# A hand-written TensorE order for the DeltaNet of a two-layer decoder trunk

## The chip, the cores and the metric

The kernel runs on one core of a Trainium2 chip. The metric is the device time of one execution in microseconds (us). The engines are named as in the profile: PE is TensorE (PEld its weight loads), DVE is VectorE, ACT is ScalarE, POOL is GpSimd, SP is SyncE, which issues most transfers. Each engine works through its own instructions in order and waits on semaphores for the others.

## The reference

Two layers, a gated DeltaNet and a latent attention, each followed by a dense SwiGLU block, all modulated by a conditioning vector (adaLN). SEQ and D_MODEL are 1024, batch 1, everything float32. The change lies in the DeltaNet of the first layer, 8 heads of 128. Cut to what matters:

```python
def gdn_mixer(h, w_in, conv_w, a_log, dt_bias, norm_g, w_out):
    proj = h @ w_in                      # per head: q, k, v, gate; and a, b for decay and beta
    qkv = jax.nn.silu(causal_depthwise_conv(qkv, conv_w))
    ...
    o = chunk_gated_delta_rule(q, k, v, g, beta)
    o = rmsnorm(o, norm_g) * jax.nn.silu(gate)
    return o.reshape(B, T, GDN_VALUE_DIM) @ w_out

def chunk_gated_delta_rule(q, k, v, g, beta):   # S_t = exp(g_t)(I - b_t k_t k_t^T) S_{t-1} + b_t k_t v_t^T
    L = jnp.where(strict, jnp.einsum("bhnid,bhnjd->bhnij", kb, k) * decay, 0.0)
    A = L + jnp.eye(C)
    u, w = triangular solves of A against v * beta and kb * exp(g_cum)
    attn = jnp.einsum("bhnid,bhnjd->bhnij", q, k) * decay
    def step(S, xs):                             # one chunk
        v_new = u_i - w_i @ S
        o_i = q_i @ S + a_i @ v_new
        S = S * gl_i + k_i^T @ v_new
```

## The kernel before

The normed and transposed input stays in SBUF, split into a high and a low fp32r half (hThi, hTlo). Each head has four projections: KT, QT, VT and ZT (the gate). One of them is 48 matmuls: two halves of 512 tokens, 8 contraction tiles, and the three products high·high, high·low, low·high (`mm3`, L195). They are written here as pj, the tile that takes them. Behind each half ACT and DVE do the convolution (taps cacc, L334) and the SiLU. The weights come as one 512 KB transfer into one of three buffers wraw; ACT makes the high half (L177), DVE the low one (L178).

The recurrence uses chunks of 128 tokens, 8 to a head. What a head needs ahead of it is prepared in two steps. `gdn_prep_a` forms K·K (L375), on DVE the sums for the norm of k (junk, L379), on POOL a power (rk), and the matrix L (L392). `gdn_prep_b` solves with L: copies of its diagonal blocks (Ld, L412, four on ACT), 31 substitution steps of two small operations on DVE (L421, L423), then per four chunks a merge: ACT copies Xs (L441), DVE makes U (L443), and four groups of matmuls follow (L447, L452, L462 with L464, L471) with copies between them. It also forms the products Q·K (L433), which DVE multiplies with the decay (at, L434).

`gdn_rec` is the recurrence. A chunk transposes K and V (L488, L489), then: K·S and Q·S (L496, L497); DVE forms r (L499); U·r (L506); ACT copies y (L508); kd·y (L511); DVE updates S (L515); at·y (L518); DVE adds to o (on, L520). Behind every fourth chunk the four pieces of o are scaled (L532), transposed (L537), gated (oT, L539) and written to DRAM. So K·S, U·r and kd·y are the links of a chain, with another engine between each two.

Around this lie the vectors of the adaLN for later phases (an ada step is one 1024-wide DVE operation, L119, behind one 512 KB transfer) and `gdn_out`, the output product of heads 0 to 3: 192 matmuls of 512 columns, each row of tokens reading o back from DRAM.

The order of all engines is the Tile scheduler's. `gdn` writes the work as tokens, A and B for the two preparations, K and V for two projections each, R for the recurrence:

```python
pre, loop, tail = "A0 V0 B0 K1 A1 V1", "B1 R0 K2 A2 V2", "B6 R5 K7 A7 V7 G0 B7 R6"
```

The loop is repeated for five heads, with the numbers raised by one each time, and the last head's R stands inside `gdn_out`. The scheduler then interleaves the instructions of neighbouring tokens on every engine by its own estimate of when each becomes ready.

Of the kernel before, what the change touches and what calls it, by code (L numbers as in the profile page):

```python
# [19 lines left out]
P = 128  # L20
# [12 lines left out]
class Trunk:  # L33
# [188 lines left out]
    def gdn_gates(self, hi, lo, pool, ps):  # L222
# [65 lines left out]
        self.split(gl, self.ghi, self.glo)  # L288
        pg = ps.tile([P, 3, N], F32, name="c")
# [11 lines left out]
    def gdn_proj(self, h, names, hi, lo, res, first=None):  # L301

        nc = self.nc
        for nm in names:
            t = {"KT": 1, "QT": 0, "VT": 2, "ZT": 3}[nm]
            ch = t * 8 + h
            if not first:
                whi, wlo = self.gdn_w(h, nm)
            o = self.gq_pool.tile([P, T], F32, name=nm, bufs=2 if nm == "ZT" else 3)
            prev = None  # L310
            for s in range(2):

                pj = first[nm][s] if first else self.pp.tile([P, 512], F32, name="pj")
                sl = slice(s * 512, s * 512 + 512)
                if not first:
                    self.mm3(pj, [(whi[:, kt], wlo[:, kt]) for kt in range(KT)],
                             [(hi[:, kt, sl], lo[:, kt, sl]) for kt in range(KT)])
                if nm == "ZT":
                    acc = self.gw.tile([P, 512], F32, name="cacc", bufs=2)
                    nc.scalar.activation(out=acc, in_=pj, func=AF.Copy, scale=0.5)  # L320
                    nc.scalar.activation(out=o[:, sl], in_=pj, func=AF.Tanh, scale=0.5)
                    nc.vector.scalar_tensor_tensor(out=o[:, sl], in0=o[:, sl], scalar=1.0, in1=acc, op0=ALU.add,
                                                   op1=ALU.mult)
                    continue
                cr = self.gw.tile([P, 515], F32, name="cr", bufs=2)
                if s == 0:
                    nc.gpsimd.memset(cr[:, 0:3], 0.0)
                else:
                    nc.gpsimd.tensor_copy(cr[:, 0:3], prev[:, 512:515])
                nc.scalar.copy(cr[:, 3:515], pj)  # L330
                acc = self.gw.tile([P, 512], F32, name="cacc", bufs=2)
                nc.scalar.activation(out=acc, in_=cr[:, 3:515], func=AF.Copy, scale=self.cw[:, 3, ch:ch + 1])  # L332
                for j in (2, 1, 0):
                    nc.vector.scalar_tensor_tensor(out=acc, in0=cr[:, j:j + 512], scalar=self.cw[:, j, ch:ch + 1],  # L334
                                                   in1=acc, op0=ALU.mult, op1=ALU.add)

                nc.scalar.activation(out=o[:, sl], in_=acc, func=AF.Tanh)
                nc.vector.scalar_tensor_tensor(out=o[:, sl], in0=o[:, sl], scalar=1.0, in1=acc, op0=ALU.add,
                                               op1=ALU.mult)
                prev = cr  # L340
            res[nm] = o
        return res
# [20 lines left out]
    def gdn_prep_a(self, h, kq):  # L363

        nc, v = self.nc, self.nc.vector
        K, Q = kq["KT"], kq["QT"]
        qq = self.gs.tile([P, NT], F32, name="qq", bufs=3)
        rkb = self.gs.tile([P, NT], F32, name="rkb", bufs=3)
        c2 = self.gs.tile([P, NT], F32, name="c2", bufs=3)
        L = self.gb.tile([P, NT, P], F32, name="L", bufs=2)  # L370
        for qd in range(2):
            pk = self.pc.tile([P, 4, P], F32, name="c")
            for i in range(4):
                cs = slice((qd * 4 + i) * P, (qd * 4 + i + 1) * P)
                nc.tensor.matmul(pk[:, i], K[:, cs], K[:, cs], start=True, stop=True)  # L375
            kd = self.gs.tile([P, 4], F32, name="kd")
            for i in range(4):
                junk = self.gw.tile([P, P], BF16, name="junk")
                v.scalar_tensor_tensor(out=junk, in0=pk[:, i], scalar=1.0, in1=self.ident, op0=ALU.mult,  # L379
                                       op1=ALU.mult, accum_out=kd[:, i:i + 1])  # L380
            v.tensor_scalar(out=kd, in0=kd, scalar1=EPS, op0=ALU.add, scalar2=None)
            rk = self.gs.tile([P, 4], F32, name="rk")
            self.rpow(rk, kd)
            ms = slice(qd * 4, qd * 4 + 4)
            gsl = slice(h * NT + qd * 4, h * NT + qd * 4 + 4)
            v.tensor_tensor(out=rkb[:, ms], in0=rk, in1=self.beta[:, gsl], op=ALU.mult)
            b2 = self.gs.tile([P, 4], F32, name="b2")
            v.tensor_tensor(out=b2, in0=rk, in1=rkb[:, ms], op=ALU.mult)
            v.scalar_tensor_tensor(out=c2[:, ms], in0=b2, scalar=-1.0, in1=self.eg[:, gsl], op0=ALU.mult, op1=ALU.mult)
            dec = self.gdn_decay(h, qd, False, "dec")  # L390
            for i in range(4):
                v.scalar_tensor_tensor(out=L[:, qd * 4 + i], in0=pk[:, i], scalar=b2[:, i:i + 1], in1=dec[:, i],  # L392
                                       op0=ALU.mult, op1=ALU.mult)
            pq = self.pc.tile([P, 4, P], F32, name="c")
            for i in range(4):
                c = qd * 4 + i
                nc.tensor.transpose(pq[:, i], Q[:, c * P:(c + 1) * P], self.ident)
            for i in range(4):
                junk = self.gw.tile([P, P], BF16, name="junk2")
                nc.scalar.activation(out=junk, in_=pq[:, i], func=AF.Square, accum_out=qq[:, qd * 4 + i:qd * 4 + i + 1])  # L400
        return dict(qq=qq, rkb=rkb, c2=c2, L=L)

    def gdn_prep_b(self, h, kq, pr):

        nc, v = self.nc, self.nc.vector
        K, Q, L = kq["KT"], kq["QT"], pr["L"]
# [17 lines left out]
        Xn = self.gw.tile([P, 8, R8, M], F32, name="Xn")  # L424
        v.transpose(out=Xn.rearrange("p c r m -> p c (r m)"), in_=X.rearrange("p i c -> p c i"))
        U = self.gb.tile([P, M, P], F32, name="U", bufs=2)
        at = self.gb.tile([P, M, P], F32, name="at", bufs=2)
        for qd in range(2):
            dec = self.gdn_decay(h, qd, True, "decT")
            pa = self.pc.tile([P, 4, P], F32, name="c")  # L430
            for i in range(4):
                cs = slice((qd * 4 + i) * P, (qd * 4 + i + 1) * P)
                nc.tensor.matmul(pa[:, i], K[:, cs], Q[:, cs], start=True, stop=True)  # L433
            v.tensor_tensor(out=at[:, qd * 4:qd * 4 + 4], in0=pa, in1=dec, op=ALU.mult)  # L434
        for m0 in range(0, M, 4):
            mh = slice(m0, m0 + 4)

            Xs = self.xs
            for b in range(4):
                pb = slice(b * 32, b * 32 + 32)  # L440
                nc.scalar.copy(Xs[pb, :, b * 32:b * 32 + 32].rearrange("p m (r c) -> p m r c", c=8),  # L441
                               Xn[pb, :, :, mh].rearrange("p c r m -> p m r c"))
            v.transpose(out=U[:, mh], in_=Xs)  # L443
            pw = self.pe.tile([P, 4, 64], F32, name="e")
            for i in range(4):
                rhs = U[:, m0 + i].rearrange("p (a b c) -> p a b c", b=2, c=32)[:, :, 1]
# [179 lines left out]
    def gdn(self, right, outer):  # L626
# [5 lines left out]
        with ExitStack() as s2:  # L632
# [875 lines left out]
```

## Time and profile before

| | us |
|---|---|
| median of 3 runs | 2617.85 |
| lowest and highest run | 2616.78, 2626.49 |
| the profiled execution | 2613.28 |
| its span | 2611.6 |
| projections and first preparation, up to the first U·r | 65 to 184 |
| first U·r to the end of the recurrence | 184 to 738 |
| FFN products of the first layer, a piece of them | 845 to 1235 |

Where the profile names a stretch, times count from the span's start. A row of the timeline gives start, length, engine, line, operation, output<-inputs and sizes; an idle time of the engine ahead of it stands in brackets with what ended it. A wait is put down to the instruction whose semaphore came last. Records of matmuls overlap, since they are pipelined.

### The profile page before, as it was taken

What the parts mean: (1) busy time and instruction counts of PE and PEld (TensorE: products, weight loads), DVE (VectorE), ACT (ScalarE), POOL (GpSimd) and SP (SyncE); (2) the same over time, 40 slices, a digit from 0 to 9 for tenths busy, and PEclk for the clock granted to TensorE, in tenths of its full rate; (3) what the DMA queues carried; (4) which work ended last, traced back from release to release, by engine and by line L of the source; (5) the groups of instructions that cost most, each with busy time, mean ns of one, the idle gap of its engine ahead of it and who ended that gap; (6) DMA issues with size and microseconds to landing.
All of it is one profiled execution on the core that took longest, in us unless ns stands there. A gap on an engine that the chain in (4) does not pass through costs nothing.

```text
span 2611.6 us, 35555 instructions
## 1 busy us (share of the span) xinstructions
PE 2505.5 (96%) x12757; PEld 2058.1 (79%) x12757; DVE 1962.5 (75%) x3748; ACT 1173.5 (45%) x2374; POOL 171.5 (7%) x322
## 2 busy tenths in 40 slices
PE   6999999999999999999999899999999999999998
PEld 5777777777778888888888798888779888887886
DVE  5787789888758888877586766668577777774778
ACT  5555454555465222322344665555283332332343
POOL 1211111221000000000000010000010000000000
PEclk8999999999999999999999999999999999999999
DMA  6111222331454544544945521112643332336634
GB/s 228 41 33 33 75 79 85 89 102 62 153 181 142 182 153 155 160 147 156 314 146 153 155 70 60 47 51 87 216 157 96 108 108 93 108 104 224 226 94 145
DMA packets 258705, 327.62 MB, mean 125 GB/s; under 512 B 17578, under 2 KB 176448, under 8 KB 258528
## 3 DMA queue, kind: packets, MB, share of 16 engines
q1 hardware_dynamic: 235840, 284.37, 34.7%
q10 hardware_dynamic: 22688, 40.97, 4.2%
q8 instruction: 101, 1.65, 0.3%
q14 instruction: 76, 0.62, 0.1%
HBM read 247.16 MB, written 78.14 MB: 125 GB/s over the span
## 4 chain that ended last, share of the span: by engine, by line
PE 77%; DVE 11%; ACT 4%; DMA 3%; issue 2%; POOL 2%; ACTq 0%; POOLq 0%; DVEq 0%; SPq 0%
PE pd L971 14%; PE nrm_p L202 14%; PE pj L202 14%; PE pd L202 10%; PE P L202 8%; PE pd L1288 3%; PE po L202 2%; DVE cacc L334 2%; PE pq L202 1%; PE tp L1331 1%; DVE X L423 1%; DVE st L421 1%; ACT Xs L441 1%; DVE wlo L178 1%; PE d L511 1%
## 5 line engine op out<-in xcount | busy, mean ns | idle before, releaser
L971 PE MATMUL pd<-wlo,gh 128*128 128x512 f32 x616 | 243.9, 396 | 2.5 <-DVE wlo L178 2.0
L971 PE MATMUL pd<-whi,gl 128*128 128x512 f32 x616 | 241.3, 393 | 0.9 <-DVE gl L178 0.9
L971 PE MATMUL pd<-whi,gh 128*128 128x512 f32 x616 | 236.9, 394 | 3.7 <-ACT gh L177 3.3
L202 PE MATMUL pj<-hThi,whi 128*128 128x512 f32 x480 | 197.0, 410 | 0.0
L202 PE MATMUL pj<-hThi,wlo 128*128 128x512 f32 x480 | 196.5, 409 | 0.0
L202 PE MATMUL pj<-hTlo,whi 128*128 128x512 f32 x480 | 196.0, 408 | 0.0
L177 ACT CAST gh<-wraw 128x1024 fp32r<-128x1024 f32 x84 | 82.3, 979 | 247.4 <-PE pd L971 209.2
L177 ACT CAST whi<-wraw 128x1024 fp32r<-128x1024 f32 (+3 forms) x105 | 100.8, 961 | 143.8 <-DMA wraw<-in_ffn_w_gate_dram 54.2
L178 DVE TENSOR_TENSOR gl<-wraw,gh 128x1024 fp32r<-128x1024 f32 x84 | 95.2, 1133 | 63.9 <-ACT gh L177 63.4
L971 PEld LDWEIGHTS pd<-wlo,gh 128*128 128x128 f32 x616 | 116.3, 189 | 33.3 <-DVE wlo L178 8.1
L219 POOL TENSOR_TENSOR nrm_r<-nrm_r,mh 128x1 f32<-128x1 f32 x56 | 37.4, 669 | 1585.3 <-DVE nrm_r L213 965.7
L971 PEld LDWEIGHTS pd<-whi,gh 128*128 128x128 f32 x616 | 116.2, 189 | 30.4 <-ACT gh L177 4.2
L178 DVE TENSOR_TENSOR wlo<-wraw,whi 128x1024 fp32r<-128x1024 f32 (+3 forms) x105 | 117.5, 1119 | 28.6 <-ACT whi L177 26.4
L971 PEld LDWEIGHTS pd<-whi,gl 128*128 128x128 f32 x616 | 116.3, 189 | 26.6 <-DVE gl L178 1.5
L202 PE MATMUL nrm_p<-T,xrow 128*128 128x512 f32 (+1 forms) x576 | 133.7, 387 | 0.0
L202 PE MATMUL nrm_p<-T,ow_hi 128*128 128x512 f32 (+1 forms) x600 | 132.0, 369 | 0.0
L202 PE MATMUL nrm_p<-T,ow_lo 128*128 128x512 f32 (+1 forms) x552 | 125.8, 376 | 0.0
L202 PEld LDWEIGHTS nrm_p<-T,xrow 128*128 128x128 f32 x576 | 105.3, 189 | 23.5
L202 PEld LDWEIGHTS nrm_p<-T,ow_hi 128*128 128x128 f32 x600 | 103.8, 189 | 20.6 <-ACT fh L791 0.2
L202 PEld LDWEIGHTS nrm_p<-T,ow_lo 128*128 128x128 f32 x552 | 98.0, 189 | 20.4
L334 DVE SCALAR_TENSOR_TENSOR cacc<-cr,cwc,cacc 128x512 f32<-128x512 f32 x144 | 108.5, 760 | 3.3 <-ACT cacc L332 2.8
L202 PEld LDWEIGHTS pj<-hTlo,whi 128*128 128x128 f32 x480 | 92.0, 192 | 15.4
(531 smaller groups left out, 6399.0 us busy)
## 6 DMA issues: line engine op xcount, KB each, us to landing
wraw<-in_ada_w_dram SPq DMA_DIRECT2D x80, 512.0 KB, 4.1
wraw<-in_ffn_w_gate_dram SPq DMA_DIRECT2D x44, 512.0 KB, 3.9
wraw<-in_ffn_w_up_dram SPq DMA_DIRECT2D x44, 512.0 KB, 4.4
gd_S<-sx ACTq DMA_DIRECT2D x88, 256.0 KB, 2.5
B<-in_ffn_w_down_dram SPq DMA_DIRECT2D x40, 512.0 KB, 6.8
wraw<-gd_S SPq DMA_DIRECT2D x40, 512.0 KB, 5.1
gd_A<-co ACTq DMA_DIRECT2D x66, 256.0 KB, 2.1
wraw<-in_gdn_w_in_dram SPq DMA_DIRECT2D x32, 512.0 KB, 4.6
```

The source lines that it names most:

```text
L177: nc.scalar.copy(hi, raw)
L178: nc.vector.tensor_tensor(out=lo, in0=raw, in1=hi.bitcast(F32), op=ALU.subtract)
L202: nc.tensor.matmul(out, l, r, start=(i == 0), stop=(i == len(seq) - 1))
L219: self.nc.gpsimd.tensor_tensor(out=out, in0=in_, in1=self.mh[:, 0:in_.shape[1]], op=ALU.pow)
L334: nc.vector.scalar_tensor_tensor(out=acc, in0=cr[:, j:j + 512], scalar=self.cw[:, j, ch:ch + 1], in1=acc, op0=ALU.mult, op1=ALU.add)
L421: v.tensor_tensor(out=t[:, 0:n], in0=Lr[:, j, j + 1:32].rearrange("p (i o) -> p i o", o=1).broadcast_to([P, n, 8]), in1=X[:, j:j + 1].broa ...
L423: v.tensor_tensor(out=X[:, j + 1:32], in0=X[:, j + 1:32], in1=t[:, 0:n], op=ALU.subtract)
L441: nc.scalar.copy(Xs[pb, :, b * 32:b * 32 + 32].rearrange("p m (r c) -> p m r c", c=8), Xn[pb, :, :, mh].rearrange("p c r m -> p m r c"))
L511: nc.tensor.matmul(psn, kd, y, start=True, stop=True)
L971: nc.tensor.matmul(acc[t], x[:, j, ts], y[:, j], start=(j0 + j == 0 and k == 0), stop=(j0 + j == NJ - 1 and k == 2))
L1288: nc.tensor.matmul(sc[:, 0:nm], q[:, ts], k[:, cs], start=(i == 0), stop=(i == 4 and not last))
L1331: nc.tensor.transpose(pt[:, kt - k0], pes[qi][:, kt * P:(kt + 1) * P], self.ident)
```

## The change

The whole DeltaNet up to the recurrence's end now stands in a new function `gdn_heads`, which runs under `tc.manual_schedule(engines={PE})`: PE's instructions keep the order in which they are written, while DVE, ACT, POOL and SP are still ordered by the scheduler. The functions are cut so that they can be interleaved: a projection is a generator that yields after every matmul (`gdn_stream`; `take(F, n)` emits n of them), the preparation is split into `gdn_kk`, `gdn_L`, `gdn_qq`, `gdn_at`, `gdn_sub` (yields after each substitution step), `gdn_diag` (Xs and U) and `gdn_merge` (yields after each of its four matmul groups), and the recurrence into `gdn_kv` (the transposes), three parts of `gdn_rec` (K·S and Q·S with r; U·r with y; kd·y and at·y, now in one bank) and `gdn_o`.

Each chunk is one frame. Besides that the gates ZT are projected one head later than before, the next projection's weights are loaded one projection ahead, the ada steps come one to a frame, with their sum in one of the three wraw buffers, K of the last chunk is no longer transposed, and the output product of heads 0 to 3 runs in the frames of head 7.

```diff
-            pre, loop, tail = "A0 V0 B0 K1 A1 V1", "B1 R0 K2 A2 V2", "B6 R5 K7 A7 V7 G0 B7 R6"
...
+            with tc.manual_schedule(engines={mybir.EngineType.PE}):
+                rest = self.gdn_heads(hi, lo, hst, right)
+            for _ in rest:
+                pass
...
+        F = self.gdn_stream([(0, "VT"), (1, "KT"), (1, "QT"), (1, "VT"), (0, "ZT")], hi, lo, self.kqv)
...
+        sub = self.gdn_sub(0)
+        take(sub, 4)
+        for i in range(7):
+            take(F, 12)
+            take(sub, 4)
+            if i in (1, 3):
+                self.gdn_at(0, i // 2)
+            if i in (4, 6):
+                self.gdn_kk(1, i // 2 - 2)
+                self.gdn_L(1, i // 2 - 2)
+        sub = self.gdn_sub(1)
+        m = self.gdn_merge(0, 0)
+        for i in range(4):
+            take(F, 8)
+            take(m)
...
+            take(sub, 3)
+        self.gdn_kv(0, 0)
+        take(F, 240)
...
+        for h in range(H):
+            names = [(h + 2, n) for n in ("KT", "QT", "VT")] if h < 5 else \
+                [(7, "KT"), (7, "QT")] if h == 5 else [(7, "VT")] if h == 6 else []
+            names += [(h + 1, "ZT")] if h < H - 1 else []
+            if names:
+                F = self.gdn_stream(names, hi, lo, self.kqv)
+            n = 12 if h < 5 else 9 if h == 5 else 8 if h == 6 else 10
+            m4 = self.gdn_merge(h, 4)
...
+            for c in range(NT):
+                self.gdn_rec(h, c, 0)
+                take(F, n)
+                self.gdn_rec(h, c, 1)
+                if c < NT - 1:
+                    self.gdn_kv(h, c + 1)
+                elif h < H - 1:
+                    self.gdn_kv(h + 1, 0)
+
+                if c == 4:
+                    self.gdn_o(h, 0)
+                if c == 0 and h > 0:
+                    self.gdn_o(h - 1, 1)
+                if c < 4:
+                    take(m4)
+                elif h < H - 1:
+                    if c == 4:
+                        m0 = self.gdn_merge(h + 1, 0)
+                    take(m0)
+                    if c == 6:
+                        self.gdn_diag(h + 1, 4)
...
+                if c in (3, 4) and h + 2 < H:
+                    self.gdn_kk(h + 2, c - 3)
+                if c in (5, 6) and h + 2 < H:
+                    self.gdn_qq(h + 2, c - 5)
+                self.gdn_rec(h, c, 2)
+                if c in (0, 1) and h + 1 < H:
+                    self.gdn_at(h + 1, c)
+                if c in (3, 4) and h + 2 < H:
+                    self.gdn_L(h + 2, c - 3)
+                take(sub, 5)
+                if c == 4 and h + 2 < H:
+                    sub = self.gdn_sub(h + 2)
+                take(ada, 1 if c != 1 or not done else 2)
+                if h == H - 2:
...
+                    if c == 5:
+                        take(F, 100)
+                        F = iter(())
...
+                if h == H - 1 and c == 0:
+                    F = self.gdn_out(gp)
+                take(F, n)
+        take(F, 24)
+        self.gdn_o(H - 1, 1)
+        return F
```

PE in a chunk of head 3, before. The numbers of the lines are those of the kernel before.

```order
L496 MATMUL d<-S,KT 128x128
L497 MATMUL d<-S,QT 128x128
L202 MATMUL pj<-hTlo,whi 128x512
L202 MATMUL pj<-hThi,wlo 128x512
L202 MATMUL pj<-hThi,whi 128x512
L506 MATMUL d<-r,U 128x128
L202 MATMUL pj<-hTlo,whi 128x512
L202 MATMUL pj<-hThi,wlo 128x512
L511 MATMUL d<-y,kdr 128x128
L518 MATMUL d<-y,at 128x128
```

The same chunk after, from the last of the 12 projection matmuls behind K·S and Q·S (now L535, L536) on. L545 is U·r, L515 and L517 are the transposes of V and K, L496 and L498 a merge step, L552 is kd·y, L558 at·y, L346 a projection matmul.

```order
L346 MATMUL pj<-hThi,wlo 128x512
L545 MATMUL d<-r,U 128x128
L515 MATMUL d<-ident,VT 128x128
L517 MATMUL d<-ident,KT 128x128
L496 MATMUL e<-U,L 64x64 x4
L498 MATMUL e<-ident,U 64x64 x4
L552 MATMUL d<-y,kdr 128x128
L558 MATMUL d<-y,at 128x128
L346 MATMUL pj<-hThi,whi 128x512
```

Between K·S and U·r there were 3 projection matmuls and there are 12; between U·r and kd·y there were 2, and now small work stands there; 12 follow at·y.

PE at the first merge of head 0 (L447), before, with the tiles' numbers. wlo_1610 and whi_1609 are the weights of ZT of head 1.

```order
L202 MATMUL pj_1643<-hThi_77,wlo_1610 128x512
L447 MATMUL e_1205<-U_1166,L_825 128x64 x4
L202 MATMUL pj_1643<-hThi_77,whi_1609 128x512
L202 MATMUL pj_1643<-hTlo_78,whi_1609 128x512
L202 MATMUL pj_1643<-hThi_77,wlo_1610 128x512
```

And after, where the merge step is L479 and whi_1105 belongs to VT of head 1.

```order
L346 MATMUL pj_1365<-hTlo_78,whi_1105 128x512
L479 MATMUL e_1437<-U_1389,L_957 128x64 x4
L346 MATMUL pj_1365<-hThi_77,wlo_1106 128x512
L346 MATMUL pj_1365<-hThi_77,whi_1105 128x512
L346 MATMUL pj_1365<-hTlo_78,whi_1105 128x512
```

The merge stood behind 279 projection matmuls and stands behind 188; up to the first U·r it was 289 and is 252.

PE in the last chunks of head 6, before. L202 on oh and ol are matmuls of the output product.

```order
L202 MATMUL pj<-whi,oh 128x512
L506 MATMUL d<-r,U 128x128
L202 MATMUL pj<-wlo,oh 128x512
L202 MATMUL pj<-whi,ol 128x512
L511 MATMUL d<-y,kdr 128x128
L518 MATMUL d<-y,at 128x128
L202 MATMUL pj<-ow_hi,oh 128x512
L202 MATMUL pj<-ow_lo,oh 128x512
```

And after, frames 6 and 7 of head 6.

```order
L535 MATMUL d<-S,KT 128x128
L536 MATMUL d<-S,QT 128x128
L545 MATMUL d<-r,U 128x128
L515 MATMUL d<-ident,VT 128x128
L496 MATMUL e<-U,L 64x64 x4
L498 MATMUL e<-ident,U 64x64 x4
L552 MATMUL d<-y,kdr 128x128
L558 MATMUL d<-y,at 128x128
L535 MATMUL d<-S,KT 128x128
L536 MATMUL d<-S,QT 128x128
L545 MATMUL d<-r,U 128x128
L515 MATMUL d<-ident,VT 128x128
```

The wide matmuls between the links are gone there; of the output product's 192 matmuls 173 stood ahead of the last U·r, and now 140 do.

## Rows read from the trace of the kernel before

**Rows 1.** The page, part 1: engine, busy us (share of the span) xinstructions.

```profile
PE 2505.5 (96%) x12757; PEld 2058.1 (79%) x12757; DVE 1962.5 (75%) x3748; ACT 1173.5 (45%) x2374; POOL 171.5 (7%) x322
```

**Rows 2.** Table of stretches: start:end, length, busy us of each engine, clock, DMA.

```profile
core 0: us, PE busy (x) PEld busy (x) DVE busy (x) ACT busy (x) POOL busy (x), PEclk, DMA share, GB/s
65.00:184.00 119.00, 114.38 (x554) 89.59 (x553) 98.17 (x268) 64.78 (x131) 26.17 (x40) 0.96 0.16 41
184.00:738.00 554.00, 521.43 (x2955) 415.04 (x2953) 456.53 (x1196) 288.57 (x786) 91.80 (x121) 0.98 0.28 85
258.10:576.40 318.30, 298.49 (x1688) 238.37 (x1687) 277.17 (x702) 167.73 (x445) 61.86 (x83) 0.99 0.29 85
650.50:703.80 53.30, 46.64 (x260) 37.03 (x259) 44.85 (x120) 24.09 (x70) 3.92 (x4) 0.94 0.56 186
845.00:1235.00 390.00, 390.00 (x1703) 316.77 (x1702) 317.22 (x463) 113.09 (x176) 0.00 (x0) 1.00 0.50 160
```

**Rows 3.** Timeline of PE in a chunk of head 3.

```profile
427.68 0.38 PE L496 MATMUL d<-S,KT 128*128 128x128 f32 x2
...
428.35 0.39 PE L202 MATMUL pj<-hThi,wlo 128*128 128x512 f32 x1
428.58 0.40 PE L202 MATMUL pj<-hThi,whi 128*128 128x512 f32 x1
428.88 0.46 PE L506 MATMUL d<-r,U 128*128 128x128 f32 x2
...
429.70 0.49 PE L511 MATMUL d<-y,kdr 128*128 128x128 f32 x2
...
431.18 0.38 PE L496 MATMUL d<-S,KT 128*128 128x128 f32 x2
```

**Rows 4.** Waits of PE and its loads, 65 to 738: total us, times, longest.

```profile
PE c L433 <- DVE at L434: 12.8, 5, 4.7
PE d L537 <- DVE on L532: 5.3, 9, 0.8
...
PE d L506 <- DVE r L499: 0.5, 1, 0.5
...
PEld d L511 <- ACT y L508: 14.9, 43, 1.4
```

**Rows 5.** Timeline around the first merge, then a stretch behind it.

```profile
164.28 0.17 DVE L423 TENSOR_TENSOR X<-X,st 128x8 f32<-128x8 f32 x1
...
167.97 0.71 DVE L443 STREAM_TRANSPOSE U<-Xs 128x512 f32<-128x512 f32 x1 [0.64 <-ACT Xs L441]
...
168.74 1.40 PE L447 MATMUL e<-U,L 128*128 128x64 f32 x8 [2.22 <-DVE U L443]
...
172.00:180.50 8.50, 8.50 (x54) 6.96 (x53) 4.88 (x10) 5.33 (x11) 3.03 (x3) 0.75 0.06 10
```

**Rows 6.** Instructions by line, DVE and ACT, 258.1 to 576.4: busy, mean ns.

```profile
L334 DVE SCALAR_TENSOR_TENSOR cacc<-cr,cwc,cacc 128x512 f32<-128x512 f32 x72 | 54.2, 754 | 1.3 <-ACT cacc L332 0.9
L119 DVE SCALAR_TENSOR_TENSOR wraw<-wraw,cact 128x1024 f32<-128x1024 f32 x28 | 36.6, 1308 | 0.0
L178 DVE TENSOR_TENSOR wlo<-wraw,whi 128x1024 fp32r<-128x1024 f32 x17 | 22.0, 1293 | 0.6 <-ACT whi L177 0.6
...
L412 ACT COPY Ld<-L 32x256 f32<-32x256 f32 x16 | 10.6, 665 | 3.4 <-DVE L L392 3.2
```

**Rows 7.** Timeline of PE, merge steps and transposes.

```profile
287.21 1.00 PE L447 MATMUL e<-U,L 128*128 128x64 f32 x8
288.05 0.28 PE L488 MATMUL d<-ident,KT 128*128 128x128 f32 x1
288.16 0.27 PE L489 MATMUL d<-ident,VT 128*128 128x128 f32 x1
...
391.47 0.68 PE L471 MATMUL e<-w,xw 64*64 64x64 f32 x8
392.07 0.49 PE L375 MATMUL c<-KT 128*128 128x128 f32 x2
```

More of the change, by code (lines that the diff above doesn't have):

```diff
@@ L325, in gdn_proj @@
[L325 to L342, printed above, removed]
+                for kt in range(KT):
+                    for j, (l, r) in enumerate(((whi, hi), (whi, lo), (wlo, hi))):
+                        self.nc.tensor.matmul(pj, l[:, kt], r[:, kt, sl], start=(kt == j == 0),
+                                              stop=(kt == KT - 1 and j == 2))
+                        if not (kt == KT - 1 and j == 2):
+                            yield
@@ new lines, in gdn_at @@
+    def gdn_at(self, h, qd):
+        nc = self.nc
+        K, Q = self.kqv[h]["KT"], self.kqv[h]["QT"]
+        if qd == 0:
+            self.pr[h]["at"] = self.gb.tile([P, NT, P], F32, name="at", bufs=2)
+        dec = self.gdn_decay(h, qd, True, "decT")
+        pa = self.pc.tile([P, 4, P], F32, name="c")
+        for i in range(4):
+            cs = slice((qd * 4 + i) * P, (qd * 4 + i + 1) * P)
+            nc.tensor.matmul(pa[:, i], K[:, cs], Q[:, cs], start=True, stop=True)
+        nc.vector.tensor_tensor(out=self.pr[h]["at"][:, qd * 4:qd * 4 + 4], in0=pa, in1=dec, op=ALU.mult)
@@ L423, in gdn_prep_b @@
             v.tensor_tensor(out=X[:, j + 1:32], in0=X[:, j + 1:32], in1=t[:, 0:n], op=ALU.subtract)
-        Xn = self.gw.tile([P, 8, R8, M], F32, name="Xn")
+            yield
+        Xn = self.pr[h]["Xn"] = self.gw.tile([P, 8, R8, M], F32, name="Xn")
         v.transpose(out=Xn.rearrange("p c r m -> p c (r m)"), in_=X.rearrange("p i c -> p c i"))
[L426 to L434, printed above, removed]
@@ new lines, in gdn_sub, with gdn_diag @@
+        self.pr[h]["U"] = self.gb.tile([P, M, P], F32, name="U", bufs=2)
+        self.gdn_diag(h, 0)
+    def gdn_diag(self, h, m0):
+        Xn, U, mh = self.pr[h]["Xn"], self.pr[h]["U"], slice(m0, m0 + 4)
+        for b in range(4):
+            pb = slice(b * 32, b * 32 + 32)
+            self.nc.scalar.copy(self.xs[pb, :, b * 32:b * 32 + 32].rearrange("p m (r c) -> p m r c", c=8),
+                                Xn[pb, :, :, mh].rearrange("p c r m -> p m r c"))
+        self.nc.vector.transpose(out=U[:, mh], in_=self.xs)
@@ L685, in gdn @@
-            pre, loop, tail = "A0 V0 B0 K1 A1 V1", "B1 R0 K2 A2 V2", "B6 R5 K7 A7 V7 G0 B7 R6"
-            for t in pre.split():
-                do(t)
-            for h in range(H - 1):
-                if h < 5:
-                    for t in loop.split():
-                        do(t[0] + str(int(t[1:]) + h))
-                elif h == 5:
-                    for t in tail.split():
-                        do(t)
-                if h in (1, 3):
-                    self.ada_cols(0, 3 + h // 2, self.pe, self.wraw, "e")
-                if h in (2, 4):
-                    self.ada_row(0, 2 if h == 2 else 5, self.pe, self.wraw, "e")
@@ L699, in gdn @@
-            hst.close()
-            self.bank = lambda: self.pp.tile([P, 512], F32, name="pj")
-            self.gdn_out(a["gdn_w_out"][0], lambda t: a["x"][0, t * P:(t + 1) * P, :], right, self.bank,
-                         lambda: self.gdn_rec(H - 1, kqv[H - 1], pr[H - 1]))
+            self.kqv, self.pr = [{} for _ in range(H)], {}
+            for nm in first:
+                o, prev = self.gdn_act(nm), None
+                for s in range(2):
+                    prev = self.gdn_conv(0, nm, s, first[nm][s], o, prev)
+                self.kqv[0][nm] = o
@@ new lines, in gdn_out, with load @@
+    def gdn_out(self, gp):
+        nc, a, sh = self.nc, self.a, [P, 4, P]
+        self.bank = lambda: self.pp.tile([P, 512], F32, name="pj")
+        def load(t):
+            x, raw = self.op.tile([P, D], F32, name="xrow"), gp.tile(sh, F32, name="or", bufs=2)
+            oh, ol = [self.op.tile(sh, F32R, name=n, bufs=2) for n in ("oh", "ol")]
+            nc.sync.dma_start(out=raw, in_=self.o_dram[:, 0:4, t * P:(t + 1) * P])
+            nc.sync.dma_start(out=x, in_=a["x"][0, t * P:(t + 1) * P, :])
+            self.split(raw, oh, ol)
+            return x, oh, ol
+        nxt = load(0)
+        for t in range(NT):
+            x, oh, ol = nxt
+            if t + 1 < NT:
+                nxt = load(t + 1)
+            for n in range(2):
+                ns = slice(n * 512, n * 512 + 512)
+                po = self.bank()
+                for i, w in enumerate(self.ws):
+                    for j, (l, r) in enumerate(((oh, w[0]), (oh, w[1]), (ol, w[0]))):
+                        nc.tensor.matmul(po, l[:, i], r[:, ns], start=(i == j == 0), stop=(i == 3 and j == 2))
+                        if not (i == 3 and j == 2):
+                            yield
+                nc.vector.tensor_tensor(out=x[:, ns], in0=x[:, ns], in1=po, op=ALU.add)
+                if n == 1:
+                    nc.sync.dma_start(out=self.x_dram[t], in_=x)
+                    if t == 2:
+                        self.ow = self.out_w((4, 5), a["gdn_w_out"][0], self.pre_gate, self.own)
+                yield
```

436 lines of the change are left out of this document (238 added, 198 removed).

## Prediction

> **What bounds the kernel now.** I read the page first: PE is 96% busy [rows 1], so time can be won only where PE waits, or where its busy time hides gaps. Only the DeltaNet's instructions are reordered, so the next view is a table of stretches [rows 2]. In the FFN (845 to 1235) PE is busy for 390.00 of 390.00 us; nothing behind the DeltaNet can gain, it only starts earlier or later. From the first U·r (184) to the end of the recurrence (738) PE is busy for 521.4 of 554.0 us: 32.6 us of visible idle time.
>
> That is a lower bound. In a run of projection matmuls the records last 0.39 us and start 0.23 us apart (428.35, 428.58 in [rows 3]), so up to 0.16 us of gap behind each is still counted as busy. The weight loads count better: in the FFN, which never waits, they fill 316.8 of 390.0 us, 0.812 of the stretch. In the recurrence they fill 415.0 us, which at 0.812 needs 511.0 us; 554.0 - 511.0 = 43.0 us are gaps by this count. I take 43 as what the waits of the recurrence are worth, with 33 as the lower end.
>
> [...] By the busy share alone the sum below would start 10 us lower and end near 2611.
>
> Who ends the waits [rows 4]: L433 (Q·K of the next head) waits for VectorE to empty a bank at L434, 12.8 us in 5 places; L537 waits for L532, 5.3; and in PE's loads kd·y waits for ScalarE's copy y, 14.9 us in 43 places. In each an instruction stands at the head of PE's queue before its operand is there.
>
> **The pre-phase, 65 to 184.** Counted in the two orders, 279 projection matmuls stand ahead of the first merge before, and 188 after: ZT0 now comes last and ZT1 is left to head 0. PE had come to that merge at 166.5 (168.74 less a wait of 2.22) [rows 5]; with 91 x 0.23 = 20.9 us less ahead of it, it comes at 145.6. U, for which the merge waits, comes from VectorE: the last substitution step of head 0 ran at 164.28, U at 167.97 for 0.71 [rows 5]. Its chain (gates, K·K, L, 62 small steps) is no shorter. VectorE loses ahead of U two weight splits of 1.29, half a projection's three taps of 0.75 [rows 6], and a little more for the gates of ZT: some 7 us. So U stands between 161 and 168.7; earlier only if VectorE's idle time shrinks too (it was 98.2 of 119.0 us busy [rows 2]), down to some 150. I take 161, which takes off the work that is gone and nothing else. PE then waits 15.4 us (4 to 23). Behind that wait stand 64 projection matmuls, before 10: 64 x 0.23 = 14.7, and some 5 for four merge steps of 0.60 to 0.84 and ten transposes of 0.11 [rows 7] with the small pieces between them: 19.7 to the first U·r. After the idle 2.22 us of before the granted clock was 0.75 over 8.5 us [rows 5], which lost 2.1; I charge 2. First U·r: 161 + 19.7 + 2 = 183, **-1 us** (-10 to +8).
>
> [...]
>
> **The recurrence.** The work between the first and the last U·r stays: 1324 wide matmuls before (1151 of projections, 173 of the output), 1328 after (1188 and 140), beside 977 and 997 small ones. So this stretch changes by its waits. What a frame has to cover stands in [rows 3]: K·S at 427.68 to U·r at 428.88 is 1.20 us; U·r to kd·y at 429.70 is 0.82; kd·y to the next K·S at 431.18 is 1.48 with other work in between. After, 12 projection matmuls (2.74 us) stand on the first link and 12 on the third. On the second stand U·r, two transposes of 0.11 and one merge step of 0.60 to 0.84 [rows 7]: over 0.82 in sum. So every link has cover, by 1.5, by some 0.1 to 0.4, and by over 1 us. L433 stands behind kd·y of frames 0 and 1, one group of four a frame, so its bank has been read. The **-43 us** go, less what the fixed order adds:
>
> *ScalarE's y*, **+6** (0 to +25). The cover of 0.1 to 0.4 is thin. ScalarE was busy 167.7 of 318.3 us in heads 1 to 4 [rows 2], and its pieces can stand ahead of y: four Ld copies of 0.67 follow one another [rows 6]. Half the time busy, with a mean rest of some 0.3 us, is 0.15 a frame, of which I leave 0.1 beyond the cover, in 56 to 64 frames. It is nearer to 0 than to 25, since the 14.9 us of rows 4 came about with less cover.
>
> *VectorE's r*, **+8** (0 to +30). In heads 1 to 4 VectorE was busy 277.2 of 318.3 us; at 75 us a head that is 92%. r has 1.5 us of slack, enough for one ada step of 1.31 or one split [rows 6] ahead of it, not for both, nor for the K·K group with a POOL power between its steps. That group falls in two frames of a head, six heads: 12 frames at 0.7 us.
>
> *The seam of heads 6 and 7*, **+5** (+3 to +12). In frames 6 and 7 of head 6 and the first half of head 7's first frame no wide matmul is left. Two and a half chunks at 1.20 + 0.82 + about 1 are 7.5 us, of which small work fills a third. That place was not full before either: 46.6 of 53.3 us at a clock of 0.94 [rows 2].
>
> **The end.** Of the 192 output matmuls of heads 0 to 3, 19 were left behind the last U·r, and now 52: 33 x 0.23 = **+7.6**. The phases after keep their instructions.
>
> **Sum.** -1 - 43 + 6 + 8 + 5 + 7.6 = -17.4. The profiled execution took 2613.28 (a span of 2611.6 and 1.7 around it), so 2595.9. The median of the runs, 2617.85, lies 4.6 above that execution: **2600.5**.
>
> **Rivals.**
>
> *(a) VectorE sets the frame.* Two in-order queues over 90% full that wait for one another once a frame keep each other's delays. The frame of heads 1 to 4 then stays at 318.3 / 32 = 9.95 us, of which VectorE's own work is 277.2 / 32 = 8.7, and some 20 of the 43 us are not won there: 2600.5 + 16 to 20, about 2618. For it speak the 8.7; against it, that only r, S and the three products' readers are due in a frame and the rest may slip.
>
> *(b) Nearly all waits go.* y and r are in time everywhere, U comes by 155, the seam costs 3: -7 - 43 + 3 + 7.6 = -39, 2578. For it: cover of 1.5 us under r; against it: the thin cover of y.
>
> *(c) Slower: r too deep in VectorE's queue.* Where r is late, PE has nothing else to take; the 12 matmuls behind U·r wait as well. -43 + 7.6 - 1 leaves 36.4 us, so this decides from 36.4 / 64 = 0.57 us a frame beyond the cover, and is slower by 0.5% from 0.77; at 0.9 it gives 2617.85 - 36.4 + 57.6 = 2639. For it: a split, an ada step whose transfer waits for one of three wraw slots (one now holds the sum), and the POOL power can all stand ahead of r. Against it: before, r cost PE 0.5 us in all [rows 4].
>
> *(d) The order is not what the code says.* The listing of the built order has the runs of 12 where the code puts them, so this gets no chance of its own.
>
> **How the numbers follow.** Forecast 0.42 (2588 to 2613 on its own), (b) 0.22, (a) 0.16, (c) 0.20. A measurement of this kernel tells some 0.5%, 13 us, from no change: faster means below 2604.8. Of the forecast's 0.42 some 0.27 lie there. Faster 0.27 + 0.22 = 0.49; within 0.15 + 0.16 = 0.31; slower 0.20. To hold 8 in 10 the range goes to just beyond (b), 2574, and into (c), 2634.
>
> **What would show it.** Right: the first U·r near 183, behind one wait of some 15 us at the first merge; heads 0 to 4 at 73 to 76 us each; L433's wait gone; the last two frames of head 6 at about 3 us each with a lower clock; the FFN as long as before. Wrong: no wait at the merge (U came in time) or one over 23; VectorE's r at the top of PE's waits, with K·S to U·r over 3 us in most frames (case c); heads 1 to 4 still at 79 (case a), or under 71 (case b).

## The result, and the profile after

The change made the kernel slower: 2708.97 us in the median (2703.33 to 2715.18) against 2621.15 before, a ratio of 1.0335 with a 95% interval of 1.0302 to 1.0367. The forecast was 2600.5, with a range up to 2634. The profiled execution took 2703.33 us, 90.0 more than before.

The page's first part and the table of stretches (start:end, length, busy us by engine, clock, DMA) answer to [rows 1, 2]. The middle stretch runs from the first to the last U·r.

```profile
PE 2531.3 (94%) x12749; PEld 2095.8 (78%) x12749; DVE 1979.5 (73%) x3748; ACT 1171.4 (43%) x2366; POOL 154.6 (6%) x322
...
65.00:192.00 127.00, 100.91 (x476) 78.41 (x475) 105.85 (x290) 60.29 (x123) 21.26 (x34) 0.92 0.11 30
192.00:812.70 620.70, 546.62 (x2984) 454.64 (x2983) 463.60 (x1170) 289.80 (x782) 78.49 (x126) 0.94 0.24 74
935.00:1325.00 390.00, 390.00 (x1702) 316.05 (x1702) 313.33 (x458) 112.34 (x174) 0.00 (x0) 1.00 0.50 158
```

The FFN is as long as before and starts 90 us later. From the first to the last U·r it is 620.7 us; before, this took 550.1 (184.0 to 734.1), with nearly the same number of wide matmuls (1324, now 1328). Of the 70.6 us, 42 are idle time (620.7 - 546.6 = 74.1, before 32.1), and 28.6 are busy time for nearly equal work, at a granted clock of 0.94 against 0.98.

PE's waits from 65 to 850 (total us, times, longest) name the place, where [rows 4] had L433 at the top:

```profile
PE d L558 <- DVE S L556: 50.6, 48, 2.2
PE e L479 <- DVE U L470: 13.8, 1, 13.8
PE d L558 <- DVE S L554: 7.7, 8, 1.2
PE d L515 <- ACT qs L541: 4.7, 5, 2.7
...
PE d L545 <- DVE r L538: 3.1, 6, 0.9
```

L558 is at·y. Before the change it waited for ScalarE's y alone, 2.7 us in 5 places. Now it waits in all 56 frames that have a kd·y until VectorE has made S: 58.3 us. It does not need S. But kd·y and at·y now lie in one PSUM tile (`po`, called a bank here), S reads kd·y's half of it, and at·y writes the other half behind that read. The timeline of PE and VectorE in frame 3 of head 3 shows what this means:

```profile
481.04 0.39 PE L552 MATMUL d<-y,kdr 128*128 128x128 f32 x2
483.21 0.49 PE L558 MATMUL d<-y,at 128*128 128x128 f32 x2 [1.78 <-DVE S L556]
...
480.48 1.28 DVE L119 SCALAR_TENSOR_TENSOR wraw<-wraw,cact 128x1024 f32<-128x1024 f32 x1 [0.82 <-DMA wraw<-in_ada_w_dram]
481.68 0.68 DVE L327 SCALAR_TENSOR_TENSOR QT<-QT,cacc 128x512 f32<-128x512 f32 x1
482.28 0.41 DVE L507 TENSOR_SCALAR U<-e 64x256 f32<-64x256 f32 x1
482.61 0.27 DVE L391 SCALAR_TENSOR_TENSOR junk<-c,ident 128x128 bf16<-128x128 f32 x1
482.82 0.08 DVE L391 DVE_READ_ACCUMULATOR junk<-c,ident 128x1 f32 x1
482.82 0.33 DVE L556 SCALAR_TENSOR_TENSOR S<-S,eg,d 128x128 f32<-128x128 f32 x1
```

kd·y starts at 481.04 and S at 482.82, behind an ada step, a SiLU, a merge copy and a norm sum that stand ahead of it on VectorE. at·y starts at 483.21, and the 12 projection matmuls that were meant to cover S stand behind at·y: PE cannot take them. The cover is on the wrong side of the wait.

The prediction has no term for this wait.

The pre-phase, answering to [rows 5]: the first merge, and two stretches around it.

```profile
170.88 1.97 PE L479 MATMUL e<-U,L 128*128 128x64 f32 x8 [13.78 <-DVE U L470]
...
157.00:171.00 14.00, 0.22 (x2) 0.12 (x1) 11.76 (x50) 4.17 (x8) 1.01 (x1) 0.62 0.00 0
171.00:180.00 9.00, 9.00 (x50) 7.62 (x51) 7.83 (x17) 5.08 (x11) 0.00 (x0) 0.80 0.22 58
```

PE stands idle for 13.8 us, and the granted clock is 0.62 in the idle stretch and 0.80 in the next.

### The profile page after: what moved, and what is told of

It is laid out like the page before. It is cut to its first block, busy times and chain, and to the rows that moved or that the text cites. A ratio compares the mean times of both kernels' runs of the same rounds, so it can differ in the third digit from the quotient of the medians.

```text
span 2701.6 us, 35351 instructions
## 1 busy us (share of the span) xinstructions
PE 2531.3 (94%) x12749; PEld 2095.8 (78%) x12749; DVE 1979.5 (73%) x3748; ACT 1171.4 (43%) x2366; POOL 154.6 (6%) x322
## 4 chain that ended last, share of the span: by engine, by line
PE 74%; DVE 14%; ACT 4%; DMA 4%; POOL 2%; issue 2%; SPq 0%; POOLq 0%; DVEq 0%; ACTq 0%
PE pd L1123 15%; PE nrm_p L202 14%; PE pd L202 9%; PE pj L202 7%; PE P L202 7%; PE pj L346 5%; PE pd L1440 3%; PE po L202 2%; DVE cacc L323 2%; PE pj L862 2%; DMA wraw<-in_ada_w_dram 2%; PE pq L202 1%; DVE X L456 1%; DVE st L454 1%; PE tp L1483 1%
## 5 line engine op out<-in xcount | busy, mean ns | idle before, releaser
L346 PE MATMUL pj<-hThi,whi 128*128 128x512 f32 x480 | 203.9, 425 | 0.0
L346 PE MATMUL pj<-hThi,wlo 128*128 128x512 f32 x480 | 196.5, 409 | 0.0
L346 PE MATMUL pj<-hTlo,whi 128*128 128x512 f32 x480 | 195.5, 407 | 0.0
L1123 PEld LDWEIGHTS pd<-whi,gh 128*128 128x128 f32 x616 | 116.6, 189 | 30.8 <-ACT gh L177 4.5
L202 PE MATMUL nrm_p<-T,xrow 128*128 128x512 f32 (+1 forms) x576 | 133.7, 386 | 0.0
L202 PE MATMUL nrm_p<-T,ow_hi 128*128 128x512 f32 (+1 forms) x600 | 132.0, 368 | 0.0
L202 PE MATMUL nrm_p<-T,ow_lo 128*128 128x512 f32 (+1 forms) x552 | 125.9, 376 | 0.0
L202 PEld LDWEIGHTS nrm_p<-T,xrow 128*128 128x128 f32 x576 | 105.1, 188 | 23.7
L202 PEld LDWEIGHTS nrm_p<-T,ow_hi 128*128 128x128 f32 x600 | 103.6, 188 | 20.7
L202 PEld LDWEIGHTS nrm_p<-T,ow_lo 128*128 128x128 f32 x552 | 97.9, 188 | 20.6
L346 PEld LDWEIGHTS pj<-hThi,wlo 128*128 128x128 f32 x480 | 94.8, 197 | 21.5
```

The source lines that it names most:

```text
L202: nc.tensor.matmul(out, l, r, start=(i == 0), stop=(i == len(seq) - 1))
L346: self.nc.tensor.matmul(pj, l[:, kt], r[:, kt, sl], start=(kt == j == 0), stop=(kt == KT - 1 and j == 2))
L1123: nc.tensor.matmul(acc[t], x[:, j, ts], y[:, j], start=(j0 + j == 0 and k == 0), stop=(j0 + j == NJ - 1 and k == 2))
```

## Experiments

Theory 1: the cost is the shared bank, at·y behind the read of S. Theory 2 is rival (a) of the prediction in a hard form: VectorE sets the frame, and a wait removed at at·y comes back at r or at K·S. The gate products (L236) begin at 80 to 82 us (79.8 before, 81.6 in the changed kernel, 81.0 in E1) or at 89 to 90 (89.3 in E2, 89.5 in E3, 88.7 in E4, 90.2 in E9, 89.4 in E11), whatever is changed behind them, and the times of most kernels lie in two groups about as far apart (E8: 2619 to 2621 and 2627 to 2629). A median of a few runs therefore depends on how many fell in each group; "from the gates" below counts from the first gate product, in the profiled execution.

**E1, two banks.**

```diff
-            po = self.pd.tile([P, 2, P], F32, name="d")
             if c < NT - 1:
-                nc.tensor.matmul(po[:, 0], self.kd, self.y, start=True, stop=True)
+                ps = self.pd.tile([P, P], F32, name="d")
+                nc.tensor.matmul(ps, self.kd, self.y, start=True, stop=True)
...
+            po = self.pd.tile([P, 2, P], F32, name="d")
             nc.tensor.matmul(po[:, 1], pr["at"][:, c], self.y, start=True, stop=True)
```

> The changed kernel, but kd·y and at·y each take a PSUM tile of their own, as they did before the change; PE's order is the same. Theory 1 (the shared bank): at·y, second in the bank, is held until VectorE's S has read kd·y's half; the 58 us of PE waiting at L558 go, and with them part of the lower clock: 60 to 85 us less than the 2709 of the changed kernel, 2625 to 2650. Theory 2 (VectorE sets the frame): the wait only moves to r or to K·S; at most 15 us less, 2694 to 2709.

2634.12 us, ratio to before 1.0065 (1.0041 to 1.0089). The waits of PE, its stretch from the first to the last U·r, and one pair of kd·y and at·y:

```profile
PE e L479 <- DVE U L470: 13.7, 1, 13.7
PE d L515 <- ACT qs L541: 9.7, 8, 2.7
PE d L545 <- DVE r L538: 6.6, 9, 2.2
PE d L559 <- ACT kdr L522: 3.8, 7, 1.6
...
193.00:744.50 551.50, 520.67 (x2983) 436.84 (x2983) 446.14 (x1170) 291.97 (x782) 79.09 (x126) 0.97 0.28 84
...
450.17 0.39 PE L552 MATMUL d<-y,kdr 128*128 128x128 f32 x2
450.39 0.39 PE L559 MATMUL d<-y,at 128*128 128x128 f32 x2
...
451.35 0.34 DVE L556 SCALAR_TENSOR_TENSOR S<-S,eg,d 128x128 f32<-128x128 f32 x1
```

The wait for S is gone. The stretch falls from 620.7 to 551.5 us: 43 of the 69 us are idle time, 26 are busy time at a clock of 0.97 instead of 0.94. Theory 2 falls: r takes 3.5 us more than with one bank, not 58, and K·S has no wait. PE's order is the same as in the changed kernel, but the scheduler has reordered VectorE around it (some 860 of the 1168 instructions of this stretch keep their sequence). That is not what removed the wait: S now starts 1.03 us in the mean behind the end of kd·y, and with one bank it was 0.65. S comes later than with one bank, and PE no longer stands still for it. Four fifths of the loss (2.7 of 3.35%) is this bank.

**E2, at·y first, bank shared.**

```diff
             po = self.pd.tile([P, 2, P], F32, name="d")
+            nc.tensor.matmul(po[:, 1], pr["at"][:, c], self.y, start=True, stop=True)
             if c < NT - 1:
                 nc.tensor.matmul(po[:, 0], self.kd, self.y, start=True, stop=True)
...
-            nc.tensor.matmul(po[:, 1], pr["at"][:, c], self.y, start=True, stop=True)
```

> The changed kernel with the bank still shared, but at·y issued ahead of kd·y, so that no matmul writes the bank behind VectorE's read of it. S comes some 0.2 us later, under 12 matmuls of cover. Theory 1 (it is the read between two writes of one bank, not the bank's use as such): 55 to 80 us less than 2709, within 8 us of the run with two banks. Theory 2 (VectorE sets the frame): 2694 to 2715.

2650.25, ratio 1.0108 (1.0075 to 1.0141). No wait for S at at·y remains, so it is the read between two writes and not the sharing. It misses the 8 us: its median is 16 above E1's. Half of that lies ahead of the gates, which begin at 89.3 in this profile and at 81.0 in E1's; from the gates to the end the two differ by 8.0 (2559.5 and 2551.5). Its r waits 10.9 us, once for 5.0.

**E3, the kernel before with one bank.**

```diff
+                po2 = self.pd.tile([P, 2, P], F32, name="d")
+                psn, po = po2[:, 0], po2[:, 1]
...
-                    psn = self.pd.tile([P, P], F32, name="d")
...
-                po = self.pd.tile([P, P], F32, name="d")
```

> The kernel before, with kd·y and at·y in one PSUM tile, nothing else; the scheduler orders all engines and puts several projection matmuls between the two. Theory 1: a wait for S appears at at·y, shortened by what stands between them: 2 to 25 us slower than 2621, so 2623 to 2646. Theory 2: no change, 2616 to 2626.

2622.23, ratio 1.0007 (0.9988 to 1.0025): no change, below what theory 1 had. In PE's weight loads the wait is there, 24 times, but short:

```profile
PEld d L518 <- DVE S L516: 5.1, 24, 0.7
```

In the built order the scheduler puts some five rows between kd·y and at·y, where none stood before. So the bank alone costs nothing that these runs can tell (the interval reaches 0.25%, 6.6 us); it costs where the order puts the two next to each other (58.3 us of waits in the changed kernel).

**E4 and E5, the scheduler's order on the new code**, E4 with the bank shared, E5 with two banks (E1's edit).

```diff
-            with tc.manual_schedule(engines={mybir.EngineType.PE}):
-                rest = self.gdn_heads(hi, lo, hst, right)
+            rest = self.gdn_heads(hi, lo, hst, right)
```

> The changed kernel's code without the hand-written order: the scheduler orders PE as well; bank shared. It places some seven rows between kd·y and at·y. Theory 1: most of the 58 us at L558 go, so 2630 to 2665; what is left above 2621 is the work's new arrangement (pre-phase, gates later, output at the end). Theory 2: the frame is VectorE's whatever the order of PE, 2690 to 2709.

> Two PSUM tiles for kd·y and at·y and the scheduler's order on PE. If the hand order costs only by the shared bank, this equals the run with two banks and the hand order (2634 then). If the hand order costs in other places too (the first merge's wait of 13.7 us), this is 15 to 30 us below that, 2604 to 2619, and within 8 us of the scheduler's order with one bank (2612), since the scheduler had already parted the two matmuls.

E4: 2612.08, ratio 0.9961 (0.9942 to 0.9980). E5: 2612.10, ratio 0.9969 (0.9953 to 0.9984). Both are faster than both kernels, than the one before by 0.3 to 0.4%, with 1 outside the interval. E4 lies below its forecast, E5 within. E4's stretch and what is left of the wait:

```profile
193.40:720.70 527.30, 503.00 (x2923) 416.27 (x2922) 442.49 (x1191) 287.17 (x776) 80.20 (x118) 0.99 0.28 86
...
PE d L558 <- DVE S L556: 2.9, 6, 1.0
```

527.3 us against 550.1 before. The stretch holds 1297 wide matmuls instead of 1324, which is 27 x 0.23 = 6.2 us; so the new arrangement of the work is worth some 17 us there, and 12 in E5 (531.6 us, again 1297). Behind the last U·r 12 us are paid again (from there to the end 1889.5, before 1877.4). Of these some may be spread between executions, since E3, with the code of before, took 1883.3. What loses is the hand-written order on top of the arrangement. When PE's order is the scheduler's, VectorE's changes too (some 920 of E1's 1168 instructions in the stretch keep their sequence in E5), so whole orders are compared here, not PE's alone.

**E6, more work ahead of the first merge** (on E1).

```diff
-        F = self.gdn_stream([(0, "VT"), (1, "KT"), (1, "QT"), (1, "VT"), (0, "ZT")], hi, lo, self.kqv)
+        F = self.gdn_stream([(0, "VT"), (1, "KT"), (1, "QT"), (1, "VT"), (0, "ZT"), (1, "ZT")], hi, lo, self.kqv)
...
-            take(F, 12)
+            take(F, 19)
...
-            names += [(h + 1, "ZT")] if h < H - 1 else []
+            names += [(h + 1, "ZT")] if 0 < h < H - 1 else []
...
-            n = 12 if h < 5 else 9 if h == 5 else 8 if h == 6 else 10
+            n = 9 if h == 0 else 12 if h < 5 else 9 if h == 5 else 8 if h == 6 else 10
```

> Hand order with two banks, and the gate projection of head 1 (48 matmuls) taken back ahead of the first merge: 19 instead of 12 matmuls in each of the seven groups, 9 a frame in head 0. Theory A (the wait at the first merge is an empty engine): the wait of 13.7 us shrinks to 2 to 4, the first U·r stays near 193, head 0 falls by some 10 us, and the time by 8 to 12 below the 2634 of two banks: 2622 to 2626. Theory B (VectorE is the bound there and is pushed back by the added work): the first U·r comes later by as much as is won, 2630 to 2638.

2639.55, ratio 1.0066 (1.0041 to 1.0091), the ratio of E1; the time lies above both bands, 1.6 us beyond theory B's. The first merge still waits:

```profile
182.54 1.97 PE L479 MATMUL e<-U,L 128*128 128x64 f32 x8 [10.10 <-DVE U L470]
```

From the gates it starts at +93.2, against +89.2 in E1: the projections added for PE push VectorE, and U with it, 4 us back, and the first U·r comes 2.7 us later (+114.8, E1 +112.1). So far this is theory B. But the wait did fall from 13.7 to 10.1 us, and from the gates to the end this profile is 6.9 us shorter than E1's (2544.6 and 2551.5). The five runs show no such gain, so whether the filling wins anything stays open.

**E7, one bank with cover in between.**

```diff
+            mid()
             nc.tensor.matmul(po[:, 1], pr["at"][:, c], self.y, start=True, stop=True)
...
-                self.gdn_rec(h, c, 2)
+                m = min(n, 6)
+                self.gdn_rec(h, c, 2, lambda: take(F, m))
...
-                take(F, n)
+                take(F, n - m)
```

> The changed kernel, bank still shared, kd·y first, but 6 of the 12 projection matmuls that follow at·y stand between kd·y and at·y. At 0.23 us each they cover 1.4 us; the waits at L558 were 1.04 us in the mean, 2.2 at most. Theory 1 (the wait is for a read that takes its time, and nothing else): all but 2 to 6 us of the 58 go, 2634 to 2645. Theory 2 (the bank's sharing costs in another way than the order): 2680 to 2709.

2655.45, ratio 1.0132 (1.0113 to 1.0151). Between the two bands, nearer to theory 1:

```profile
PE d L559 <- DVE S L556: 12.7, 13, 2.5
```

Some 46 of the 58 us are gone, where all but 2 to 6 were expected; 1.4 us of cover are not enough in 13 frames, and the longest wait that is left, 2.5 us, is longer than any in the changed kernel (2.2). When S comes depends on what stands ahead of it on VectorE, which that cover does not shorten.

**E8, two banks, hand order in the loop over heads alone.** The `with` of E4 is taken away and one is opened ahead of the loop.

> Two banks; the hand order only from the loop over the heads on, the work ahead of it in the scheduler's order. If the frames are as good by hand as by the scheduler and only the pre-phase is worse, this is as fast as the scheduler's order throughout, 2608 to 2616. If the frames by hand are slower too, it stays between, 2618 to 2630.

2623.99, ratio 1.0019 (1.0004 to 1.0034): between. Of the 0.96% from E1 to E5, the order of the pre-phase is half (1.0065 to 1.0019) and the order of the frames the other (1.0019 to 0.9969).

**E9, K·K and L of head 1 behind the first merge** (on E1).

```diff
-            if i in (4, 6):
-                self.gdn_kk(1, i // 2 - 2)
-                self.gdn_L(1, i // 2 - 2)
...
-            take(sub, 3)
+            if i < 2:
+                self.gdn_kk(1, i)
+                self.gdn_L(1, i)
+            else:
+                take(sub, 6)
```

> Hand order with two banks; K·K and L of head 1 are moved from ahead of the first merge of head 0 to between its steps, and the substitution of head 1 starts two steps later with six steps at a time. This takes some 6 to 8 us of VectorE's work (8 products at 0.28, 8 at 0.34, their small steps and two waits for a POOL power) from ahead of U. Theory B (VectorE is the bound of the pre-phase): U stands 5 to 8 us sooner than 170.2, the wait of 13.7 shrinks by as much, the first U·r comes 4 to 8 us sooner than 193.1. If the chain of 62 small steps alone sets U, nothing moves: 192 to 194.

2634.08, ratio 1.0046 (1.0030 to 1.0063). The three kernels' gate products (first to last start), the first step of the substitution (Lr) and the first merge, in the order before, E1, E9:

```profile
L236 PE MATMUL c<-hThi,at x16: 390/392/399, 79.8 to 86.8; 128*32 128x512 f32 x16
...
120.91 1.25 DVE L414 STREAM_TRANSPOSE Lr<-Ld 128x1024 f32<-128x1024 f32 x1 [1.39 <-ACT Ld L412]
```

```profile
L236 PE MATMUL c<-hThi,at x16: 388/397/628, 81.0 to 89.5; 128*32 128x512 f32 x16
...
129.42 1.25 DVE L447 STREAM_TRANSPOSE Lr<-Ld 128x1024 f32<-128x1024 f32 x1 [1.81 <-ACT Ld L445]
...
170.23 1.97 PE L479 MATMUL e<-U,L 128*128 128x64 f32 x8 [13.74 <-DVE U L470]
```

```profile
L236 PE MATMUL c<-hThi,at x16: 390/392/628, 90.2 to 98.7; 128*32 128x512 f32 x16
...
138.60 1.25 DVE L447 STREAM_TRANSPOSE Lr<-Ld 128x1024 f32<-128x1024 f32 x1 [1.82 <-ACT Ld L445]
...
172.90 1.97 PE L479 MATMUL e<-U,L 128*128 128x64 f32 x8 [17.87 <-DVE U L470]
```

From the gates the merge comes at +88.9 before (168.74 in [rows 5]), +89.2 in E1, +82.7 in E9: 6.5 us sooner, as theory B had it. The first U·r comes 4 us sooner (+108.1, E1 +112.1), the end 2.9. The ratio's interval overlaps E1's, so the gain in time is not shown. The wait itself is longer in E9, since PE, too, has less to do ahead of it.

**E10, the transposes' tile from the merge's banks** (on E1).

```diff
-        pt = self.pd.tile([P, 2, P], F32, name="d")
+        pt = self.pe.tile([P, 2, P], F32, name="e")
```

> Hand order with two banks; the transposes of K and V take their tile from the merge's pair of banks instead of the recurrence's pair. With two banks their place was the one that ScalarE's qs still reads: 9.7 us of waits at L515 in 8 places. If that pair of banks is what the hand-written frames still lack, the waits at L515 go and the time falls by 5 to 12 us from 2634, to 2622 to 2629. If a bank is merely waited for elsewhere (the merge's own copies), no change, 2630 to 2640.

2642.88, ratio 1.0074 (1.0048 to 1.0099). The time lies 2.9 us above the second case's band, and from the gates to the end the profile is 6.9 us longer than E1's (2558.4). The wait has moved, as the second case had it:

```profile
PE e L498 <- ACT vs L518: 10.2, 6, 2.4
```

**E11, E9 with Q's transposes and squares of head 0 moved behind the start of the substitution.**

> The kernel with two banks and the late K·K of head 1, and besides the Q transposes and squares of head 0 (four transposes and eight ScalarE pieces in each of two places) moved from between the two K·K groups to behind the start of the substitution. Theory A (the first substitution starts 7.3 us later than before because the hand order and ScalarE's squares stand ahead of the second L): it starts 2 to 4 us sooner, counted from the first gate product (48.4 us in both hand-ordered runs, 41.1 before); the first merge follows by as much (82.7 then), and the time falls by 1 to 4 us from 2634. Theory B: the start hangs on the gates alone; 48 again and no change.

2632.98, ratio 1.0057 (1.0038 to 1.0076). The substitution starts at +47.6 from the gates, 0.8 sooner, where 2 to 4 were expected, and the merge 0.7 sooner. So ScalarE's squares and Q's transposes are at most 0.8 us of the delay; what the rest is, in the order from gates to L, stays open. The time, 1.1 us below E9's, shows no gain.

## Why the prediction was wrong, step by step

**The step that failed** is the recurrence's cover of the links. It priced K·S to U·r, U·r to kd·y and kd·y to K·S, and let "12 on the third" link cover S. It took at·y for a product that waits for y alone. The edit "kd·y and at·y, now in one bank" stood in the description of the change and got no term: nobody asked who reads that bank between the two writes. E1 and E2 remove this read from between and lose the wait; E1 is 75 us faster for it. Rival (c) put the slow side at r, with a price of 0.57 us a frame to decide and 0.9 for 2639. The time lost was 58.3 / 56 = 1.04 us a frame of waiting and the clock on top, but at at·y; r itself waited 3.1 us.

**The 43 us** were mis-sized as well. With the bank parted (E1) the stretch from the first to the last U·r is 551.5 us against 550.1; forecast was 24 less. Idle time is 30.8 us against 32.1. L433's waits are all but gone, as forecast (2.3 us at Q·K, now L434), and others have come: qs 9.7, r 6.6, kdr 3.8. Heads 0 to 4 gained 17 us, 375.3 against 392.4, and heads 5 to 7 lost as much (before, then E1):

```profile
576.40:734.10 157.70, 147.41 (x840) 116.83 (x839) 119.45 (x322) 78.44 (x227) 17.93 (x21) 0.97 0.32 108
...
568.40:744.50 176.10, 161.20 (x909) 134.13 (x908) 123.25 (x317) 82.87 (x232) 19.00 (x26) 0.93 0.30 98
```

Part of these 18.4 us is work that moved there (69 records on PE, 8 of them wide matmuls); the rest is 4.6 us of idle time and a clock of 0.93 against 0.97. For these heads alone the prediction had the seam's +5 and no more. The scale was also wrong. From the weight loads I had read 43 us of gaps, but in E1 nearly the same number of loads (2983, before 2938) fills 436.8 us, before 412.7; their busy time is no fixed cost of the work. In these runs a difference of two shares of the weight loads was no measure of what an order can win. E4 and E5 show that some 12 to 17 us could be had there, with the scheduler's order.

**VectorE's r** (+8) measured 3.1 with one bank and 6.6 with two: right in size. **ScalarE's y** (+6) was charged too much: L552 waits 2.3 us for it with one bank and 0.7 with two. The 3.8 us at L559 in E1 are another wait, of at·y's new tile for the bank that ScalarE's kdr still reads. **Heads 0 to 4** were forecast at 73 to 76 us. With one bank they took 80.6, 85.1, 85.2, 88.8 and 84.5; with two, 71.6, 77.6, 76.1, 75.5 and 74.5, a mean of 75.1. So the price of these heads' frames was right but for the bank.

**The seam** was forecast at +5, with frames of 3 us at a lower clock. In E1 frame 6 of head 6 took 8.1 us (680.68 to 688.75) and frame 7 2.9; the lower clock is as forecast, 0.50 in the last row below. The long frame comes from ScalarE's qs, which stands behind three casts of output weights and two pieces of the gate on ScalarE (PE's wait, and the stretch behind it):

```profile
683.83 0.47 PE L515 MATMUL d<-ident,VT 128*128 128x128 f32 x1 [2.67 <-ACT qs L541]
...
684.00:692.00 8.00, 7.54 (x37) 5.85 (x37) 3.79 (x8) 3.63 (x11) 0.00 (x0) 0.50 0.81 274
```

**The pre-phase** was forecast with the first merge at 161, when U is there, behind a wait of 15.4, and the first U·r at 183; measured were 170.9, 13.8 and 192.1. The wait was right and the time was not. From its first step the substitution took 40.8 us to the first merge, before 47.8: the 7 us that I took off are there. But it starts 7.3 us later (+48.4 from the gates, before +41.1): in the hand order K·K of head 0 begins 1.9 us later from the gates, and its second L ends 7 us later. The count from the gates is rough by up to 3.9 us here, since the scheduler's orders have 65 wide matmuls ahead of the gates and the hand order 48; with the scheduler's order on the new code (E4) the substitution starts at +44.6. Where the prediction says that the chain "is no shorter", it should have asked when the chain starts. E6 and E9 show that VectorE's work ahead of U moves U; that filling PE helps is not shown. The clock's 2 us came: 0.62 in the idle stretch and 0.80 over the next 9.0 us, which loses 1.8 (an estimate: 9.0 x 0.20).

**The end**, +7.6, measured 1888.9 from the last U·r against 1877.4: +11.4; right in kind, and not sized better than by E3's 1883.3 for the code of before.

## What to carry to other kernels

When an edit puts two matmuls into one PSUM bank, ask who reads the first result and whether the second write is issued behind that read; in the hand-written order here it waited for the reader and for all that stood ahead of the reader on its engine, 58.3 us in 56 frames. With six matmuls between the two, 12.7 us of this were left (E7); with at·y first (E2) or a bank for each (E1), no wait of at·y for S was left; and the scheduler, which parted the two, hid the mistake (5.1 us of waits in PE's weight loads in E3, 2.9 us on PE in E4). Price a hand-written order against the scheduler's order on the same code, since regrouped work can gain and the order lose, as here: 2612 against 2634 with the bank mended.

## What the runs showed of the hardware

The short waits cost twice here. With one bank the idle time of the recurrence grew by 43 us over E1, and the same matmuls were busy for 26 us longer, at a granted clock of 0.94 against 0.97. Without the waits (E1) both were gone. The clock's ratio accounts for some 17 of the 26 us (an estimate: 520.7 x 0.97 / 0.94 - 520.7); what the other 9 are is not shown. And the time from the start to the first gate product was 79.8 us in one profiled execution and 89.5 in another whose code is the same up to there (before and E3), so that two profiles are best compared from a common instruction:

```profile
L236 PE MATMUL c<-hThi,at x16: 387/396/397, 89.5 to 96.5; 128*32 128x512 f32 x16
```
